# A two-layer decoder trunk on one core, with its instruction order worked out by the framework's finer model of engines and queues

## The chip, the core and the metric

The kernel runs on one core of a Trainium2 chip. A core has a matrix engine (TensorE, PE in the profile), three engines for elementwise work (VectorE = DVE, ScalarE = ACT, GpSimd = POOL) and SyncE (SP), whose queue here issues every DMA. Each engine takes its own instructions in the order in which they stand in its list, and waits at the head of that list for what the head instruction needs. The metric is device time in microseconds (us) of the whole program, median over runs; lower is better.

## The reference, cut to what matters

The model has two layers with 256 tokens and 2048 channels, all in 32-bit floats. Each layer is a token mixer and a SwiGLU feed-forward network (FFN), and both are modulated by a conditioning vector `c`:

```
c_act = silu(c)
for l in range(2):
    mod = c_act @ w_mod[l] + b_mod[l]                  # 2048 -> 6 * 2048
    shift1, scale1, gate1, shift2, scale2, gate2 = split(mod, 6)
    h = rms_norm(x) * (1 + scale1) + shift1
    x = x + gate1 * mixer(h, w_in[l], ..., w_out[l])    # three head groups in parallel
    h = rms_norm(x) * (1 + scale2) + shift2
    x = x + gate2 * ((silu(h @ w_gate[l]) * (h @ w_up[l])) @ w_down[l])
return rms_norm(x)
```

The mixer's three groups are gated linear attention (`gla`), sliding-window attention (`swa`) and a gated delta rule (`gdn`). The delta rule inverts a triangular matrix in a series of dependent small products. Per layer the weights hold 40.1 MB (`w_in`), 16.8 MB (`w_out`), 138 MB (gate, up and down) and 100.7 MB (`w_mod`, 2048 x 12288), so that a quarter of the bytes that the kernel reads serve only the vector `mod`.

## The kernel before

**Weights for TensorE.** `stream` (line 293 on) handles every large product. It walks over weight tiles of 128 rows and 1024 columns, 512 KB each. A tile is loaded by SP into `raw` (line 323, three buffers). ACT makes its rounded part `wh` (line 330, three buffers) and DVE the remainder `wl` (line 331, three buffers). TensorE then runs twelve products per tile (line 358): two column halves, two blocks of 128 tokens, three terms. A `raw` buffer is free again once its `wl` is made. In layer 0's mixer most tiles are used whole (`whole`): they skip the split, land in any of the `raw`, `wh` and `wl` buffers, and cost TensorE one slower product in place of three.

**The modulation vector.** `mod_segment` (line 201 on) handles `c_act @ w_mod`. DVE multiplies a loaded tile of `w_mod` with one value of `c_act` per row and adds it to `acc` (line 223). In the first part (shift1 and scale1 of layer 0) the tiles are 512 columns wide and take buffers of the mixer's pool (`g`, 256 KB, line 220). All others are 1024 columns wide and have two buffers of their own (`mraw`, 512 KB, line 220); their sums have two buffers (`acc`). Sixteen such tiles make a segment, which TensorE and ACT or DVE then finish (lines 234 to 256, `fin`).

**What sets the order.** The kernel calls its operations in one sequence. `tick` (line 273) is called after each weight tile and puts steps of the modulation between them, at a rate set by hand for each stage (`RATE_IN`, `RATE_FFN` and so on). The framework's scheduler then takes this sequence, plays the instructions through a model of the machine, and from it makes the list of each engine: an instruction whose inputs and buffers are there in the model may pass an earlier one that is still waiting. No semaphore, buffer or instruction is written out by hand; the lists follow from the model.

Stages by time in the profiled execution: first modulation segments until 41 us, layer 0's input projections and mixer until about 575 us, its FFN until about 1372 us, layer 1's projections and mixer until about 1816 us, and its FFN to the end. The gdn's inversion (lines 673 to 692, in `gdn`) is made of rounds of four small products (line 678), a masked copy on DVE (680), four products (685), a subtraction on DVE (686), four transposes (403) and a copy on ACT (687).

The few lines on which the steps rest:

```
rawp = tile_pool(name="rawp", bufs=3)       # weight tiles as loaded
modp = tile_pool(name="modp", bufs=2)       # w_mod tiles, "mraw"
wsp  = tile_pool(name="wsp", bufs=3)        # wh and wl, three each
accp = tile_pool(name="accp", bufs=2)       # sums of two segments
SY.dma_start(raw, w_mod[...])               # line 220
V.scalar_tensor_tensor(acc, raw, c_act, acc, mult, add)   # line 223
SY.dma_start(raw, w[k])                     # line 323
A.activation(wh, raw, Copy)                 # line 330
V.tensor_tensor(wl, raw, wh, subtract)      # line 331
TE.matmul(ps, x, wh or wl)                  # line 358
```

The function that the change touches:

## Time and profile before

| | us |
|---|---|
| median of 3 runs (2581.72 to 2582.03) | 2581.92 |
| the profiled execution, whole | 2585.34 |
| its span, first to last instruction | 2583.5 |
| TensorE busy in the span | 2432.7 (94%) |
| DVE busy | 1714.4 (66%) |
| ACT busy | 1053.5 (41%) |

The DMA engines read 596.63 MB, on average 232 GB/s over the span. Idle time is counted by engine; a view by time windows gives for each stretch how long each engine was busy, how many instructions it ran (x...), the share of time in which the sixteen DMA engines were busy, and the rate in GB/s. The same view for one tile's name counts only the instructions that touch that tile: `mraw` on DVE counts the modulation's products, `raw` on DVE counts the weight splits.

### The profile page before, as it was taken

How to read it: one execution, taken by the hardware profiler on the slowest of the kernel's cores; microseconds unless marked ns; L12 is line 12 of the kernel's file. 1: busy time of each engine (PE TensorE's matmuls, PEld its weight loads, DVE VectorE, ACT ScalarE, POOL GpSimd, SP SyncE). 2: the span in 40 equal slices, each digit the busy share in tenths (PEclk: the TensorE clock that was granted, in tenths of full speed). 3: DMA queues.
4: the chain of work that ended last, by engine and by line, in shares of the span. 5: the costliest groups of instructions: out<-in, count | busy, mean ns of one | idle time of the engine just before them, and what ended most of it. 6: DMA issues, size and time to landing. Idle time of an engine off the chain costs nothing.

```text
span 2583.5 us, 30803 instructions
## 1 busy us (share of the span) xinstructions
PE 2432.7 (94%) x11164; PEld 1884.1 (73%) x11164; DVE 1714.4 (66%) x2171; ACT 1053.5 (41%) x1548; POOL 58.2 (2%) x117
## 2 busy tenths in 40 slices
PE   4999998889999988999999999999999999999998
PEld 2555785447878767788877878877778878888876
DVE  6767867576675777657578785888664575544555
ACT  2203443124444333344335454564644434344443
POOL 1000000000000000000000000000000000000000
PEclk9999999989999999999999999999999999999999
DMA  9996538777778888868687861675676686666654
GB/s 341 368 322 204 180 114 282 258 231 268 261 259 260 283 268 274 292 193 286 223 277 261 281 192 50 214 232 192 212 256 193 200 286 195 188 191 188 189 184 155
DMA packets 190033, 600.79 MB, mean 233 GB/s; under 512 B 21628, under 2 KB 26268, under 8 KB 189496
## 3 DMA queue, kind: packets, MB, share of 16 engines
q1 hardware_dynamic: 189880, 598.81, 70.7%
q8 instruction: 88, 1.44, 0.2%
q14 instruction: 65, 0.53, 0.1%
HBM read 596.63 MB, written 2.10 MB: 232 GB/s over the span
## 4 chain that ended last, share of the span: by engine, by line
PE 57%; DMA 20%; DVE 10%; issue 8%; ACT 4%; POOL 1%; SPq 1%; DVEq 0%; ACTq 0%; POOLq 0%
PE acc L358 48%; DMA mraw<-in_w_mod 13%; DVE wl L331 4%; DMA raw<-in_w_down 3%; DMA raw<-in_w_in 2%; DVE acc L223 2%; ACT wh L330 1%; PE mm L403 1%; PE ga L895 1%; DMA raw<-in_w_up 1%; PE mm L678 1%; PE mm L685 1%; PE ga L916 1%; DMA raw<-in_w_gate 1%; PE fin L248 1%
## 5 line engine op out<-in xcount | busy, mean ns | idle before, releaser
L358 PE MATMUL acc<-wh,hm 128*128 128x512 f32 (+3 forms) x4872 | 1339.2, 389 | 20.9 <-DVE xs L931 4.7
L330 ACT ACTIVATE wh<-raw 128x1024 fp32r<-128x1024 f32 (+3 forms) x669 | 684.7, 1025 | 985.8 <-PE acc L358 548.9
L331 DVE TENSOR_TENSOR wl<-raw,wh 128x1024 fp32r<-128x1024 f32 (+3 forms) x669 | 785.2, 1179 | 446.6 <-ACT wh L330 444.5
L358 PEld LDWEIGHTS acc<-wh,hm 128*128 128x128 f32 x4872 | 892.0, 189 | 215.8 <-issue 25.5
L358 PE MATMUL acc<-wl,hm 128*128 128x512 f32 (+3 forms) x2484 | 792.3, 394 | 12.2 <-DVE wl L331 9.7
L223 DVE SCALAR_TENSOR_TENSOR acc<-mraw,c_act,acc 128x1024 f32<-128x1024 f32 x320 | 410.3, 1282 | 225.2 <-DMA mraw<-in_w_mod 222.9
L358 PEld LDWEIGHTS acc<-wl,hm 128*128 128x128 f32 x2484 | 458.4, 190 | 124.1 <-DVE wl L331 22.3
L358 PE MATMUL acc<-wh,ahl 128*128 128x512 f32 x560 | 158.4, 397 | 0.0
L358 PEld LDWEIGHTS acc<-wh,ahl 128*128 128x128 f32 x560 | 105.8, 189 | 24.5
L358 PE MATMUL acc<-wl,ahl 128*128 128x512 f32 x280 | 90.8, 398 | 7.2 <-DVE wl L331 7.2
L223 DVE SCALAR_TENSOR_TENSOR g<-g,c_act,g 128x512 f32<-128x512 f32 x128 | 88.7, 747 | 12.6 <-DMA g<-in_w_mod 12.4
L358 PE MATMUL acc<-wh,b 128*128 128x512 f32 (+2 forms) x184 | 74.7, 545 | 2.2 <-ACT b L447 2.1
L358 PE MATMUL acc<-wl,b 128*128 128x512 f32 (+2 forms) x176 | 67.1, 518 | 2.6 <-DVE g L969 2.6
L358 PEld LDWEIGHTS acc<-wl,ahl 128*128 128x128 f32 x280 | 52.2, 189 | 23.1 <-DVE wl L331 11.3
L358 PE MATMUL acc<-raw,b 128*128 128x512 f32 (+2 forms) x176 | 67.6, 524 | 0.0
L358 PEld LDWEIGHTS acc<-wh,b 128*128 128x128 f32 x184 | 35.2, 197 | 30.8 <-issue 23.1
L358 PEld LDWEIGHTS acc<-wl,b 128*128 128x128 f32 x176 | 32.8, 192 | 29.2 <-issue 20.3
L416 ACT ACTIVATE acc<-xs 128x512 f32<-128x512 f32 x32 | 19.0, 595 | 85.7 <-DVE xs L931 85.7
L447 ACT ACTIVATE b<-mm,mod,mod 128x128 f32<-128x128 f32 x24 | 9.2, 461 | 109.7 <-DVE mod L256 92.1
L358 PEld LDWEIGHTS acc<-raw,b 128*128 128x128 f32 x176 | 33.5, 195 | 26.7 <-issue 21.7
L929 DVE TENSOR_TENSOR acc<-acc,gate 128x512 f32<-128x512 f32 x64 | 43.0, 695 | 10.3 <-PE acc L358 10.2
L358 PE MATMUL acc<-raw,hm 128*128 128x512 f32 x88 | 41.7, 598 | 1.4 <-ACT acc L416 1.4
(314 smaller groups left out, 1645.8 us busy)
## 6 DMA issues: line engine op xcount, KB each, us to landing
mraw<-in_w_mod SPq DMA_DIRECT2D x320, 512.0 KB
raw<-in_w_down SPq DMA_DIRECT2D x176, 512.0 KB
raw<-in_w_gate SPq DMA_DIRECT2D x160, 512.0 KB
raw<-in_w_up SPq DMA_DIRECT2D x160, 512.0 KB
raw<-in_w_in SPq DMA_DIRECT2D x72, 512.0 KB
g<-in_w_mod SPq DMA_DIRECT2D x128, 256.0 KB
raw<-in_w_out SPq DMA_DIRECT2D x43, 512.0 KB
raw<-in_w_in SPq DMA_DIRECT2D x32, 264.0 KB
```

Of the source, the lines that this page charges most:

```text
L223: V.scalar_tensor_tensor(acc, raw[:, a], c_act[:, i + a:i + a + 1], acc, ALU.mult, ALU.add)
L248: TE.transpose(ps[:, i * P:(i + 1) * P], acc[:, (j + i) * P:(j + i + 1) * P], ident)
L330: A.activation(wh[:, :width], raw[:, :width], AF.Copy)
L331: V.tensor_tensor(wl[:, :width], raw[:, :width], wh[:, :width].bitcast(F32), ALU.subtract)
L358: TE.matmul(ps[blk, j][:, :segs[j][2]], xa, parts[j][part], start=i == 0 and n == 0, stop=last and n == len(terms) - 1)
L403: TE.transpose(ps[:, j * P:(j + 1) * P], src[:, j * P:(j + 1) * P], ident)
L416: A.activation(scr[0]() if junk is None else junk, xs[:, blk, j * 512:(j + 1) * 512], AF.Square, accum_out=ssq[blk][:, j:j + 1])
L678: TE.matmul(ps[:, s], LT[blk][:, s], Tm[blk][:, s], start=True, stop=True)
L685: TE.matmul(ps[:, s], U[blk][:, s], m1[:, s], start=True, stop=True)
L895: TE.matmul(ps[:, j * nk:(j + 1) * nk], qT[rows, i + j], kT[rows, g, :nk], start=True, stop=True)
L916: TE.matmul(ps[:, j * 64:(j + 1) * 64], pT[:, j * nk + kb * P:j * nk + (kb + 1) * P], kv[kb][:, P + g * 64:P + (g + 1) * 64], start=kb == ...
L929: V.tensor_tensor(ps, ps, need(gate_row, (l, part, j)), ALU.mult)
```

## The change

```diff
-    with tile.TileContext(nc) as tc:
+    with tile.TileContext(nc, schedule_with_timeline_sim=True) as tc:
         trunk(tc, *args)
```

On SP's list, at the very start: loads for the first modulation segments (`g`, from `w_mod`) and the first weights (`wh`, `wl`, `raw`, from `w_in`). Before:

```order
L220 DMA g_60_232<-in_w_mod 128x512
L220 DMA g_61_235<-in_w_mod 128x512
L220 DMA g_62_238<-in_w_mod 128x512
L220 DMA g_63_241<-in_w_mod 128x512
L220 DMA g_64_244<-in_w_mod 128x512
L220 DMA g_65_247<-in_w_mod 128x512
```

Now:

```order
L220 DMA g_60_232<-in_w_mod 128x512
L323 DMA wh_96_347<-in_w_in 128x1024
L323 DMA wl_106_372<-in_w_in 128x1024
L323 DMA raw_110_387<-in_w_in 128x1024
L323 DMA wh_114_402<-in_w_in 128x1024
L323 DMA wl_119_424<-in_w_in 128x520
L220 DMA g_61_235<-in_w_mod 128x512
```

Before, all 32 `g` loads of the first two segments stood ahead of the first weight. Now ten loads of `w_in` (3.55 MB) and four of `mraw` (2.1 MB) stand among them.

On SP's list in layer 0's FFN, at the gate projection that was read at about 780 us: weight tiles (`raw`) and the modulation's tiles (`mraw`). Before:

```order
L323 DMA raw_1339_5553<-in_w_gate 128x1024
L323 DMA raw_1342_5571<-in_w_gate 128x1024
L323 DMA raw_1345_5589<-in_w_gate 128x1024
L323 DMA raw_1355_5628<-in_w_gate 128x1024
L323 DMA raw_1358_5646<-in_w_gate 128x1024
L323 DMA raw_1362_5667<-in_w_gate 128x1024
```

Now:

```order
L323 DMA raw_1339_5553<-in_w_gate 128x1024
L220 DMA mraw_1564_6710<-in_w_mod 128x1024
L323 DMA raw_1342_5571<-in_w_gate 128x1024
L213 DMA acc_1663_7259<-in_b_mod 1x1024
L220 DMA mraw_1574_6767<-in_w_mod 128x1024
L323 DMA raw_1345_5589<-in_w_gate 128x1024
L220 DMA mraw_1581_6806<-in_w_mod 128x1024
L323 DMA raw_1355_5628<-in_w_gate 128x1024
L220 DMA mraw_1591_6863<-in_w_mod 128x1024
L323 DMA raw_1358_5646<-in_w_gate 128x1024
```

The modulation's tiles now come one for nearly every weight tile. From `raw_1065` (read at 596 us) to `raw_1964` (at 1234 us) the list held 110 `mraw` loads and now holds 181, beside the same weights: 171.0 MB before, 208.2 MB now. From layer 1's first input weight (`raw_2158`) to its first gate weight (`raw_3129`) it held 64 and now holds none. The whole lists hold the same loads.

On TensorE's list in layer 0's gdn, one round of the inversion and the beginning of the next (`mm`: the round's products; `acc` from `wh` and `wl`: input projections; `ga`: attention). Before:

```order
L678 MATMUL mm_476_1719<-g_470_1693,g_466_1681 128x128 x4
L358 MATMUL acc_678_2497<-wh_702_2608,hm_289_993 128x512
L358 MATMUL acc_679_2498<-wh_702_2608,hm_289_993 128x512
L358 MATMUL acc_676_2493<-wh_706_2629,hm_190_657 128x512
L358 MATMUL acc_677_2494<-wh_706_2629,hm_190_657 128x512
L358 MATMUL acc_676_2493<-wl_707_2630,hm_190_657 128x512
L685 MATMUL mm_478_1726<-g_477_1724,g_469_1690 128x128 x4
```

Now:

```order
L678 MATMUL mm_476_1719<-g_470_1693,g_466_1681 128x128 x4
L916 MATMUL ga_608_2247<-kv_151_533,b_606_2240 128x64
L916 MATMUL ga_608_2247<-kv_152_538,b_606_2240 128x64
L916 MATMUL ga_608_2247<-kv_151_533,b_606_2240 128x64
L916 MATMUL ga_608_2247<-kv_152_538,b_606_2240 128x64
L685 MATMUL mm_478_1726<-g_477_1724,g_469_1690 128x128 x4
L895 MATMUL ga_610_2255<-kT_412_1425,b_585_2170 128x256 x2
```

The input projections that stood between the rounds now all stand ahead of the first of them. From the first round's products to the gdn's last transposes TensorE's list held 118 products of projections, and now holds 26 (of `w_out`). On DVE's list the same rounds held 9 modulation products and now hold 31.

## The prediction

> **What bounds the kernel now.** I read the page first: TensorE's share, the slices and the chain that ended last.

> ```profile
> span 2583.5 us, 30803 instructions
> PE 2432.7 (94%) x11164; PEld 1884.1 (73%) x11164; DVE 1714.4 (66%) x2171; ACT 1053.5 (41%) x1548; POOL 58.2 (2%) x117
> GB/s 341 368 322 204 180 114 282 258 231 268 261 259 260 283 268 274 292 193 286 223 277 261 281 192 50 214 232 192 212 256 193 200 286 195 188 191 188 189 184 155
> PE 57%; DMA 20%; DVE 10%; issue 8%; ACT 4%; POOL 1%; SPq 1%; DVEq 0%; ACTq 0%; POOLq 0%
> PE acc L358 48%; DMA mraw<-in_w_mod 13%; DVE wl L331 4%; DMA raw<-in_w_down 3%; DMA raw<-in_w_in 2%; DVE acc L223 2%; ACT wh L330 1%; PE mm L403 1%; PE ga L895 1%; DMA raw<-in_w_up 1%; PE mm L678 1%; PE mm L685 1%; PE ga L916 1%; DMA raw<-in_w_gate 1%; PE fin L248 1%
> ```

> TensorE is busy 94% of the span, so a better order can win at most 150 us. The second link of the chain matters here: 13% of it is the landing of `mraw`, tiles that no weight product needs soon. A change of order moves exactly these tiles. So I cut the program into stages, and counted the modulation's products in them (the same view, for `mraw` alone) and the weight splits (for `raw` alone).

> ```profile
> core 0: us, PE busy (x) PEld busy (x) DVE busy (x) ACT busy (x) POOL busy (x), PEclk, DMA share, GB/s
> 40.80:228.00 187.20, 183.75 (x554) 101.21 (x554) 132.96 (x239) 30.37 (x68) 2.73 (x16) 0.99 0.95 337
> 371.00:575.00 204.00, 180.92 (x759) 105.16 (x760) 144.87 (x202) 52.58 (x114) 7.94 (x8) 0.96 0.80 263
> 596.00:861.00 265.00, 256.11 (x1131) 206.76 (x1130) 179.13 (x161) 113.05 (x121) 1.91 (x2) 1.00 0.82 274
> 861.00:1041.00 180.00, 165.54 (x702) 131.08 (x701) 128.56 (x122) 61.01 (x61) 1.90 (x2) 0.97 0.83 271
> 1372.00:1694.00 322.00, 309.49 (x1853) 260.76 (x1853) 241.81 (x401) 166.04 (x319) 13.95 (x31) 1.00 0.62 199
> 1694.00:1816.00 122.00, 112.73 (x582) 88.08 (x582) 102.69 (x146) 67.49 (x114) 4.46 (x4) 0.99 0.62 204
> 596.00:1245.00 649.00, 623.52 (x2732) 503.26 (x2731) 438.08 (x399) 259.69 (x270) 4.77 (x5) 0.99 0.81 268
> ```

> Modulation products (`mraw`), three stages, then weight splits (`raw`):

> ```profile
> 861.00:1041.00 180.00, 0.00 (x0) 0.00 (x0) 47.47 (x37) 0.00 (x0) 0.00 (x0) 0.97 0.83 271
> 1372.00:1694.00 322.00, 0.71 (x2) 0.30 (x2) 64.52 (x52) 1.25 (x2) 0.00 (x0) 1.00 0.62 199
> 1694.00:1816.00 122.00, 1.98 (x6) 1.05 (x6) 19.22 (x16) 1.16 (x2) 0.00 (x0) 0.99 0.62 204
> ...
> 861.00:1041.00 180.00, 0.00 (x0) 0.00 (x0) 68.89 (x57) 59.22 (x57) 0.97 0.83 271
> 2150.00:2550.00 400.00, 0.00 (x0) 0.00 (x0) 174.95 (x144) 151.37 (x143) 1.00 0.61 189
> ```

> The last row is the pace that TensorE sets when nothing disturbs it: 144 tiles in 400 us, 2.78 us per weight tile, at 189 GB/s. In 861 to 1041 us, 57 tiles took 180 us, 3.16 us each, with 37 modulation tiles beside them. TensorE ran 702 products there; in 2150 to 2550 it runs 1761 in 400 us, so 792 in 180. A ninth was lost. The rate was only 271 GB/s. Why it is no higher, the timeline of that stretch shows:

> ```profile
> 886.95 0.33 SPq L323 DMA_DIRECT2D raw<-in_w_down  x1
> 890.42 1.28 DVE L223 SCALAR_TENSOR_TENSOR acc<-mraw,c_act,acc 128x1024 f32<-128x1024 f32 x1 [3.49 <-DMA mraw<-in_w_mod]
> 891.73 0.33 SPq L220 DMA_DIRECT2D mraw<-in_w_mod  x1
> 891.94 1.06 ACT L330 ACTIVATE wh<-raw 128x1024 fp32r<-128x1024 f32 x1 [1.70 <-DMA raw<-in_w_down]
> 893.22 1.28 DVE L223 SCALAR_TENSOR_TENSOR acc<-mraw,c_act,acc 128x1024 f32<-128x1024 f32 x1 [0.38 <-DMA mraw<-in_w_mod]
> 894.42 1.22 DVE L331 TENSOR_TENSOR wl<-raw,wh 128x1024 fp32r<-128x1024 f32 x1
> ```

> SP issued nothing from 887.3 to 891.7 us: the next load on its list, an `mraw`, waited for DVE to free its buffer, and DVE had waited 3.49 us for the `mraw` before it. The weight loaded at 886.95 landed by 891.94, ACT took 1.06, and its `wl` stood behind a modulation product until 894.42, so the buffer was free at 895.64: 8.7 us round trip for one of three buffers. The loop of five buffers through SP's and DVE's strict lists sets the rate, not TensorE. SP's waits in nearly the same window say it in sum:

> ```profile
> SPq L323 <- DVE wl L331: 120.5, 61, 4.2
> SPq L220 <- DVE acc L223: 13.3, 12, 1.4
> ```

> **The change, part by part.** The sum is made against the profiled execution (2585.3 us with what lies around its span), which is 3.4 us above the median of the runs shown.

> 1. *Start.* The first product on weights is here:

> ```profile
> 5.32 26.05 SPq L220 DMA_DIRECT2D g<-in_w_mod  x31
> 40.83 2.08 PE L358 MATMUL acc<-wh,b 128*128 128x512 f32 x2 [2.09 <-ACT b L447]
> ```

> It needs the last of 32 `g` loads. The new list puts 5.65 MB ahead of that load. At the second slice's 368 GB/s that is 15 us; if the weights only fill time in which SP waited for `g` buffers, the 2.1 MB of `mraw` remain, 6 us. TensorE is then full (183.75 of 187.20 us in the first row of the stage table), so what is lost stays lost until some idle time takes it back. I take +10 (6 to 15).

> 2. *Layer 0's mixer.* The gdn's rounds lose their cover: 118 - 26 = 92 products of the projections now run earlier, and 22 more modulation products stand between the rounds on DVE. Their price if each holds the chain up, by the 1.28 us above, is 28 us; with 92 products of 0.23 us (400 us / 1761) uncovered, 21 more, together 49. Against that, 371 to 575 us has 23 us of idle TensorE, where `w_out` waited; those products come earlier in the new list, too. What runs earlier is no less work, so a gain is bounded by these 23. I take +5 (-20 to +49), near nothing since DVE's load over the stage is the same.

> 3. *Layer 0's FFN, 596 to 1245 us.* The same weights (221 splits) now come with 181 modulation tiles for 110: 208.2 MB. If the rate stays the 271 GB/s of the stretch that is most like it, this takes 768 us for 649: +119. If the queue can be filled to a share of 1.00, the rate is 271 / 0.83 = 327 GB/s and the stage takes 637 us: -12. The best single window that TensorE filled is this:

> ```profile
> 1170.00:1235.00 65.00, 64.98 (x295) 53.63 (x294) 51.11 (x47) 27.07 (x28) 0.00 (x0) 1.00 0.90 302
> ```

> Sustained 302 would give 689 us, +40. I take the mean of 271 and 302, 286 GB/s: 728 us, +79. DVE gets 71 more products, 91 us on 438 of 649: no bound by itself, but each stands ahead of some `wl`. What waits behind a late `wl` is SP's next weight load three tiles on.

> [...]

> 4. *Rest of layer 0's FFN (1245 to 1372 us):* 9 `mraw` loads for 14. -5 (-8 to 0).

> 5. *Layer 1's mixer (1372 to 1816 us):* its modulation is done already. 68 products go, 84 us of DVE's 344. TensorE idles 22 us by the two rows; the norms and the gdn chain keep a part of it. Here, too, the projections move ahead of the last rounds. -10 (-22 to +15).

> 6. *Layer 1's FFN* keeps its 32 modulation tiles in all, a little earlier; 0. From 2150 us on the lists load the same tiles in the same order; that stretch must not change.

> Sum: 10 + 5 + 79 - 5 - 10 = +79. 2585.3 + 79 = 2664, less 3.4 is **2661 us**.

> **The rivals.**

> *A. The loop is not the limit (faster).* With an `mraw` always next to a weight, all five buffers are in flight and the rate goes up, as it did at the start (337 GB/s over 187 us, where the loads had more buffers). Break-even is 208.2 MB / 649 us = 321 GB/s; above it TensorE's pace decides, 221 x 2.78 = 614 us, -35. For it: the DMA share of 0.83 leaves room. Against: that share already went with 271 GB/s. At 327 GB/s: +10 + 0 - 12 - 5 - 20 = -27, about 2555 us by the median.

> *B. The bare gdn chains cost, too (slower still).* Each modulation product between two rounds waits for its tile's landing, and with it DVE and the chain. Layer 0 then pays its 49 instead of 5, layer 1 gains nothing: 79 + 44 + 10 = 133, 2715 us. For it: 22 more products among the rounds. Against: one attention block's work still lies between them.

> *C. Gains and losses meet.* At 308 GB/s the FFN loses 27 (676 us) and its rest gains 5; layer 1 gains its 22, the start costs 6 and layer 0's mixer gains 6: 0, 2582 us. For it: all terms but one are small.

> That the lists don't differ is excluded: they do.

> **How the numbers follow.** The forecast's case has 0.68, A 0.12, B 0.16, C 0.04. The likeliest case alone runs from 2610 (FFN at 302 GB/s, layer 1 at its best) to 2700 (271 GB/s). With C below and the larger part of B above, 8 in 10 lie in 2580 to 2730. A change under 0.2%, 5 us, is about what this measurement can't tell from none. Faster: A, 0.12 (C's sides cancel). Same: C, 0.04. Slower: 0.84.

> **What would show it.** In the new profile, layer 0's FFN (to be found by its first gate weight and layer 1's first `w_in` weight) should be some 75 us longer; its windows should show 275 to 300 GB/s, TensorE near 85%, and ACT's `wh` waiting for the landing of `raw`. The first product on weights should start near 51 us. Layer 1's mixer should show no `mraw` and a rate under 140 GB/s. The last 430 us should look as before. If layer 0's FFN shows over 320 GB/s and a full TensorE, step 3 is wrong and the kernel is faster; if the FFN is as predicted and the total is not, the mixers' steps are.

## The result, and the profile after

The changed kernel is slower: 2720.19 us (median of 4 runs, 2717.2 to 2721.98) against 2581.82 us, a ratio of 1.054 (95% interval 1.0522 to 1.0559). The forecast was 2661 us in a range of 2580 to 2730: the sign and the range hold, the sum is 59 us short. The profiled execution took 2720.07 us.

The page of the changed kernel gives the span and the engines' busy time:

```profile
span 2718.3 us, 30932 instructions
PE 2484.0 (91%) x11164; PEld 1946.1 (72%) x11164; DVE 1719.4 (63%) x2171; ACT 1058.8 (39%) x1551; POOL 55.8 (2%) x117
```

The span grew by 134.8 us. TensorE ran the same 11164 instructions, but was busy 51.3 us longer (2484.0 for 2432.7). So it was idle 83.5 us longer, and what it ran took longer. The mean clock that TensorE was granted fell from 0.986 of the full one to 0.959. The prediction had no term for that second part.

To see where the time went I take the start of the first product that uses the same weight tile, in both traces:

| up to the first product on | before, us | after, us | stretch longer by |
|---|---|---|---|
| the first weight tile | 40.8 | 55.7 | +15 |
| a tile late in layer 0's projections (`wl_675`) | 237.7 | 258.6 | +6 |
| layer 0's second gate pair (`raw_1065`): the mixer | 603.4 | 666.3 | +42 |
| `raw_1964`: most of layer 0's FFN | 1245.0 | 1342.3 | +34 |
| layer 1's first input weight (`raw_2158`) | 1372.5 | 1475.3 | +6 |
| layer 1's first gate weight (`raw_3129`): the mixer | 1816.5 | 1940.1 | +21 |
| near the end (`raw_4067`) | 2526.7 | 2662.9 | +13 |

Windows of the kernel before over layer 0's mixer and FFN (us, busy time of PE, PEld, DVE, ACT, POOL with counts, then clock, DMA share, GB/s):

```profile
238.00:603.00 365.00, 331.94 (x1618) 225.88 (x1616) 256.59 (x408) 131.43 (x299) 19.23 (x24) 0.95 0.63 203
603.00:1245.00 642.00, 617.38 (x2704) 498.52 (x2705) 433.50 (x395) 258.03 (x269) 4.77 (x5) 0.99 0.81 268
```

The same stages of the changed kernel, and layer 1's mixer in two pieces:

```profile
259.00:666.00 407.00, 353.91 (x1625) 252.14 (x1624) 248.58 (x407) 143.13 (x311) 18.95 (x24) 0.89 0.53 168
666.00:1342.00 676.00, 629.78 (x2747) 511.36 (x2746) 523.82 (x481) 258.01 (x269) 10.51 (x11) 0.97 0.89 308
1475.00:1700.00 225.00, 222.43 (x1203) 189.96 (x1203) 130.59 (x240) 121.60 (x201) 4.16 (x5) 0.98 0.54 153
1700.00:1940.00 240.00, 211.15 (x1208) 174.18 (x1206) 139.40 (x235) 109.39 (x222) 6.17 (x13) 0.93 0.31 95
```

Three things stand in these rows. Layer 0's mixer holds nearly the same products and takes 42 us more: 22 of them are TensorE's products at a lower clock (353.91 us at 0.89 for 331.94 at 0.95; if the busy time goes with the clock, I estimate from these rows 315 us at a clock of 1.00 for both), 20 are idle. Layer 0's FFN moves 308 GB/s, more than the 286 that the forecast took, so it loses less. In layer 1's mixer TensorE is nearly full for 225 us, and idle for 29 of the 240 us behind them, at a clock of 0.93; its projections are used up by 1735 us, and the products of `w_out` start near 1795. (The sizes at the head of this document make `w_mod` 201 of the 597 MB that are read: a third, not a quarter.)

The 20 idle us lie in the rounds of layer 0's inversion, from the first product of line 678 to the last. These rounds in the kernel before:

```profile
288.60:344.90 56.30, 56.30 (x383) 48.00 (x382) 40.15 (x57) 24.47 (x52) 2.14 (x5) 1.00 0.40 122
```

and in the changed kernel, with DVE's longest wait there (us in total, times, longest):

```profile
374.40:458.20 83.80, 63.70 (x362) 49.85 (x361) 61.26 (x77) 17.93 (x47) 2.99 (x7) 0.88 0.69 210
DVE acc L223 <- DMA mraw<-in_w_mod: 19.0, 22, 2.3
```

The rounds take 84 us for 56. Among them DVE now runs 30 modulation products (38.5 us; 7 before) and waits 19 us for the landing of their tiles (not at all before). Its busy time and these waits fill 80 of the 84 us.

### The profile page after: what moved, and what is told of

The parts are those of the page before. It is cut to its first block, busy times and chain, and to the rows that moved or that the text cites. A ratio compares the mean times of both kernels' runs of the same rounds, so it can differ in the third digit from the quotient of the medians.

```text
span 2718.3 us, 30932 instructions
## 1 busy us (share of the span) xinstructions
PE 2484.0 (91%) x11164; PEld 1946.1 (72%) x11164; DVE 1719.4 (63%) x2171; ACT 1058.8 (39%) x1551; POOL 55.8 (2%) x117
## 4 chain that ended last, share of the span: by engine, by line
PE 56%; DMA 23%; DVE 11%; ACT 5%; issue 4%; SPq 0%; POOL 0%; DVEq 0%; ACTq 0%; POOLq 0%
PE acc L358 49%; DMA mraw<-in_w_mod 15%; DVE acc L223 4%; DVE wl L331 3%; ACT wh L330 2%; DMA raw<-in_w_up 2%; DMA raw<-in_w_down 2%; DMA raw<-in_w_gate 1%; DMA g<-in_w_mod 1%; DMA raw<-in_w_in 1%; DVE acc L929 1%; PE mm L403 1%; PE ga L895 1%; DVE g L223 1%; PE ga L403 1%
## 5 line engine op out<-in xcount | busy, mean ns | idle before, releaser
L358 PE MATMUL acc<-wh,hm 128*128 128x512 f32 (+3 forms) x4872 | 1357.7, 391 | 32.9 <-DVE xs L931 17.1
L331 DVE TENSOR_TENSOR wl<-raw,wh 128x1024 fp32r<-128x1024 f32 (+3 forms) x669 | 785.4, 1179 | 530.1 <-ACT wh L330 527.1
L358 PEld LDWEIGHTS acc<-wh,hm 128*128 128x128 f32 x4872 | 906.3, 191 | 234.5 <-issue 39.1
L330 ACT ACTIVATE wh<-raw 128x1024 fp32r<-128x1024 f32 (+3 forms) x669 | 683.8, 1026 | 985.8 <-PE acc L358 499.1
L358 PE MATMUL acc<-wl,hm 128*128 128x512 f32 (+3 forms) x2484 | 808.6, 395 | 9.8 <-DVE wl L331 8.1
L358 PEld LDWEIGHTS acc<-wl,hm 128*128 128x128 f32 x2484 | 464.8, 192 | 120.2 <-issue 17.1
L223 DVE SCALAR_TENSOR_TENSOR acc<-mraw,c_act,acc 128x1024 f32<-128x1024 f32 x320 | 410.2, 1282 | 158.0 <-DMA mraw<-in_w_mod 156.2
L358 PE MATMUL acc<-wh,ahl 128*128 128x512 f32 x560 | 156.4, 395 | 0.0
L358 PEld LDWEIGHTS acc<-wh,ahl 128*128 128x128 f32 x560 | 105.5, 188 | 24.7
L223 DVE SCALAR_TENSOR_TENSOR g<-g,c_act,g 128x512 f32<-128x512 f32 x128 | 89.7, 746 | 19.5 <-DMA g<-in_w_mod 13.6
L358 PE MATMUL acc<-wl,ahl 128*128 128x512 f32 x280 | 90.5, 397 | 0.8 <-DVE wl L331 0.8
L358 PE MATMUL acc<-wh,b 128*128 128x512 f32 (+2 forms) x184 | 78.1, 535 | 4.0 <-ACT b L447 4.0
L358 PE MATMUL acc<-raw,b 128*128 128x512 f32 (+2 forms) x176 | 73.2, 526 | 2.0 <-ACT b L447 1.5
L358 PE MATMUL acc<-wl,b 128*128 128x512 f32 (+2 forms) x176 | 72.5, 522 | 1.5 <-ACT b L447 1.5
L358 PEld LDWEIGHTS acc<-wl,ahl 128*128 128x128 f32 x280 | 52.1, 188 | 14.6 <-DVE wl L331 2.8
L358 PEld LDWEIGHTS acc<-wh,b 128*128 128x128 f32 x184 | 35.4, 194 | 34.2 <-issue 26.5
L358 PEld LDWEIGHTS acc<-raw,b 128*128 128x128 f32 x176 | 33.5, 193 | 29.5 <-issue 23.8
L358 PEld LDWEIGHTS acc<-wl,b 128*128 128x128 f32 x176 | 33.6, 195 | 27.9 <-issue 23.2
L447 ACT ACTIVATE b<-mm,mod,mod 128x128 f32<-128x128 f32 x24 | 9.0, 457 | 102.6 <-DVE mod L256 98.7
L358 PE MATMUL acc<-raw,hm 128*128 128x512 f32 x88 | 42.9, 611 | 0.0
L931 DVE TENSOR_TENSOR xs<-xs,acc 128x512 f32<-128x512 f32 x64 | 41.7, 680 | 0.3
```

The costliest lines, as they stand in the source:

```text
L223: V.scalar_tensor_tensor(acc, raw[:, a], c_act[:, i + a:i + a + 1], acc, ALU.mult, ALU.add)
L330: A.activation(wh[:, :width], raw[:, :width], AF.Copy)
L331: V.tensor_tensor(wl[:, :width], raw[:, :width], wh[:, :width].bitcast(F32), ALU.subtract)
L358: TE.matmul(ps[blk, j][:, :segs[j][2]], xa, parts[j][part], start=i == 0 and n == 0, stop=last and n == len(terms) - 1)
L447: A.activation(h32[:, i], ps[:, i * P:(i + 1) * P], AF.Identity, scale=mod_col[l, 3 * sub + 1, at + i], bias=mod_col[l, 3 * sub, at + i])
L931: V.tensor_tensor(x_j, x_j, ps, ALU.add)
```

## The experiments

Most runs fix the order of issue on some engines. Every instruction has the same name in all these programs, so an engine's list can be taken from one kernel and laid on another: each instruction is tied behind the one ahead of it on its engine, an order of issue without a wait. Engines that are not tied get their lists from the finer model, worked out anew beside the tied ones; such a list need not be the changed kernel's.

```diff
+    known = {i.name: i for i in nc.cur_bb.bb.instructions}
+    for packed in lists:
...
+        for a, b in zip(names, names[1:]):
+            tc.add_manual_dep(known[b], a, mybir.DependencyInfo(
+                mybir.DependencyClass.NoSync, mybir.DependencyReason.DATA), reason="pin")
```

All results by stage, against the kernel before, in us and in the stretches of the table above (start and projections; layer 0's mixer; its FFN; the FFN's rest; layer 1's mixer; its FFN), with the ratio of times:

| run | start | mixer 0 | FFN 0 | rest | mixer 1 | FFN 1 | ratio (95%) |
|---|---|---|---|---|---|---|---|
| the change | +21 | +42 | +34 | +6 | +21 | +13 | 1.054 (1.0522 to 1.0559) |
| loads_before | 0 | +71 | +26 | +13 | +79 | +16 | 1.0748 (1.0723 to 1.0773) |
| pe_before_mods_free | +53 | +17 | +19 | +5 | +2 | +5 | 1.0434 (1.0402 to 1.0465) |
| pe_before | +28 | +34 | -5 | +6 | +45 | +2 | 1.0446 (1.0422 to 1.047) |
| products_in_call_order | +43 | +46 | +15 | +4 | +34 | +15 | 1.0656 (1.0624 to 1.0688) |
| only_PE_free | +9 | +76 | +2 | +5 | +60 | +16 | 1.0666 (1.0623 to 1.071) |
| only_DVE_free | +6 | +35 | +12 | +10 | +49 | +14 | 1.0493 (1.0463 to 1.0523) |
| only_mod_products_free | +5 | +24 | +16 | +9 | +27 | +6 | 1.0333 (1.0315 to 1.0351) |
| only_other_DVE_free | +3 | +19 | -1 | +1 | +18 | +10 | 1.0187 (1.0166 to 1.0208) |
| mod_products_in_call_order | +10 | +134 | -21 | +1 | +72 | +8 | 1.0792 (1.0769 to 1.0814) |
| only_SP_free | +15 | +5 | -30 | -2 | -2 | 0 | 0.9967 (0.9948 to 0.9986) |
| start_before_rest_of_SP_free | +13 | +1 | -25 | -3 | +3 | -2 | 0.994 (0.9924 to 0.9956) |
| SP_free_from_the_FFN_on | -2 | -1 | -29 | -2 | +1 | -1 | 0.9867 (0.9844 to 0.9891) |

**First: loads against TensorE's order.** Three runs, all with the finer model for what is not tied.

```diff
+        pin(tc, nc, (SP_BEFORE,))
```

> The order in which SP issues the loads is that of the kernel before, instruction for instruction; the other lists are worked out by the finer model, so that TensorE's input projections still run ahead of the delta rule's rounds (20 projection products among layer 0's rounds, against 74 before and 16 in the changed kernel). Theory 1, from the two traces: the start (+15), the K-block stage (+6) and layer 0's FFN (+34) lose by the order of the loads, and the two mixers (+42 and +21) by the bare rounds. Then the first three go and the mixers' 63 us stay: 2635 to 2670 us. Rival, as in the prediction: all that is lost hangs on the modulation's loads, and bare rounds cost next to nothing: 2580 to 2600 us.

Measured: 2778.94 us. The start is back (first weight product at 39.9 us), so the start's loss is made by the loads' order. But the whole became slower than the changed kernel. The mixers lose 150 us, and the FFN loses 26 with every load where it stood before. Neither theory had that: the old list of loads, with the lists that the finer model works out around it, is slower than both kernels.

```diff
+        pin(tc, nc, (PE_BEFORE,))
```

Here `PE_BEFORE` leaves the products of lines 238 and 248 (`fin`) out.

> TensorE's list is that of the kernel before in all but the 160 small products that finish a modulation segment; the rest is by the finer model. The rounds of the delta rule have their cover of projections again (74 products, as before), while the modulation's loads stand nearly as in the changed kernel: 179 of them in layer 0's FFN against 181 (110 before), none in layer 1's mixer, 27 modulation products on DVE among layer 0's rounds against 30. Theory 1: start, K-blocks and FFN keep their loss of about 55 us, the mixers lose little: 2635 to 2670 us. Rival (the loads' order is all): 2700 to 2725 us. If modulation products among the rounds are what stretches layer 0's mixer, not the lack of cover, its 42 us stay and the time is near 2685 us.

Measured: 2697.37 us. The mixers fall to +17 and +2, from +42 and +21, with nearly the changed kernel's modulation. So 44 of the mixers' 63 us go with TensorE's old list, in which the projections stand among layer 0's rounds again. In layer 0 this gives back the clock, and not the idle time. This run's windows over layer 0's mixer, over its rounds, and over what lies behind them:

```profile
291.00:674.00 383.00, 330.72 (x1613) 224.31 (x1612) 224.81 (x370) 130.45 (x292) 16.91 (x23) 0.95 0.51 160
363.60:445.60 82.00, 63.96 (x395) 51.75 (x394) 65.43 (x81) 22.69 (x48) 2.66 (x4) 0.96 0.67 209
445.60:674.10 228.50, 214.68 (x987) 135.67 (x986) 97.42 (x182) 84.12 (x192) 7.83 (x13) 1.00 0.39 123
```

and the changed kernel behind its rounds:

```profile
458.20:666.30 208.10, 179.80 (x673) 114.35 (x673) 95.56 (x169) 64.93 (x149) 7.05 (x9) 0.85 0.34 108
```

TensorE is busy for 330.72 us at 0.95, as in the kernel before (331.94), not 353.91 at 0.89. But it is idle for 52 us, as in the changed kernel (53; 33 before), and the rounds take 82 us with their cover of projections, for 84 without: DVE has 28 modulation products in them and waits 15.8 us for the tiles. So their length does not come from the missing cover. The start, 32 us worse than the changed kernel's, ate about half of what the other stages gained.

```diff
+        pin(tc, nc, (PE_BEFORE,))
```

> TensorE's whole list is that of the kernel before, the small products that finish a modulation segment among them; SP, DVE and ACT are ordered by the finer model. Since a segment's buffer comes free only behind those products, the loads fall back to nearly their old places (112 in layer 0's FFN, 62 in layer 1's mixer); what stays of the change is the start, with 20 modulation tiles ahead of time, and DVE's and ACT's order. Theory 1: start and K-blocks only, 2590 to 2610 us. Rival: the finer model's order on DVE (the splits against the modulation's products) costs by itself in every stage: over 2620 us.

Measured: 2699.64 us, against theory 1. TensorE's list is the old one to the last instruction, the loads are nearly back, and yet the mixers lose 34 and 45 us. Layer 0's rounds are not where: without a modulation product among them they are as short as in the kernel before.

```profile
332.80:389.20 56.40, 56.30 (x383) 47.92 (x382) 30.07 (x47) 23.35 (x50) 1.21 (x4) 1.00 0.19 57
```

This run and the one before it issue TensorE's products in the same order, all but the `fin` products. So 26 us of the rounds go with the modulation products on DVE. The clock over this run's whole mixer is 0.93, so the cover alone does not keep it up. What the mixers still lose here points to DVE's or ACT's order.

**Second: one engine at a time.** TensorE's list of the changed kernel holds something that the prediction had missed: 4570 of the 8616 weight products stand out of the sequence in which the kernel calls them (464 before).

```diff
-                TE.matmul(ps[blk, j][:, :segs[j][2]], xa, parts[j][part],
-                          start=i == 0 and n == 0, stop=last and n == len(terms) - 1)
+                put = TE.matmul(ps[blk, j][:, :segs[j][2]], xa, parts[j][part],
+                                start=i == 0 and n == 0, stop=last and n == len(terms) - 1)
+                if prods:
+                    tc.add_manual_dep(put.ins, prods.pop().name, mybir.DependencyInfo(
+                        mybir.DependencyClass.NoSync, mybir.DependencyReason.DATA), reason="pin")
+                prods.append(put.ins)
```

> The changed kernel, with one constraint: TensorE issues the weight products (line 358) in the sequence in which the kernel calls them. The finer model had moved 4570 of the 8616 from their place in that sequence (464 in the kernel before); at a group's first tiles it does one column half of three tiles in a row, and holds all three tiles' buffers open. Everything else stays as in the changed kernel, nearly: 180 modulation loads in layer 0's FFN, none in layer 1's mixer, the input projections ahead of the delta rule's rounds. Theory 2, new: the moved products cost layer 0's FFN most of its 29 us, and some of the mixers': 2680 to 2700 us, FFN (first gate weight to the layer's last-but-one weight tile) 10 us or less above the kernel before. Rival, step 3 of the prediction: the 71 additional modulation tiles cost the FFN its time; it keeps 25 to 35 us, and the whole stays at 2710 to 2725 us.

Measured: 2748.8 us. The FFN did as theory 2 says in kind (+15 for +34, with 180 modulation tiles still), but the start lost 22 us more and layer 1's mixer 13, so the whole is slower. The moved products cost the FFN some 19 us; undoing them cost more elsewhere, and the mixers kept their loss.

```diff
+        pin(tc, nc, (DVE_BEFORE, ACT_BEFORE, SP_BEFORE))
```

> SP's, DVE's and ACT's lists are those of the kernel before, instruction for instruction; TensorE's alone is worked out by the finer model. It keeps the projections among the delta rule's rounds (the other lists tie them), but moves 4884 of the 8616 weight products from their call order. Theory 2: this alone costs layer 0's FFN 10 to 25 us and the kernel 20 to 50: 2600 to 2635 us. Rival: the sequence of products within a tile or two is indifferent, since their sum is the same: 2580 to 2590 us.

Measured: 2752.69 us, far beyond both. The freed list stays near the old one, with the projections still among the rounds, and yet it costs the mixers 136 us (the FFN 2).

```diff
+        pin(tc, nc, (PE_BEFORE, SP_BEFORE, ACT_BEFORE))
```

> TensorE's, SP's and ACT's lists are those of the kernel before; DVE's alone is worked out by the finer model, which sets modulation products and attention work ahead of the delta rule's convolution (line 548) and of weight splits, by two places on average. Theory 3: DVE's order is what stretches the mixers even where TensorE's list is the old one (they lost 37 and 38 us in the run with TensorE's whole list as before): 2605 to 2650 us, with the loss in the two mixers. Rival: two places are too little to matter: 2580 to 2590 us, and the mixers' loss in that run came from the loads and ACT.

Measured: 2706.4 us. DVE's list moved by under two places on average, and the kernel lost 125 us, in all stages. The mixers' loss is theory 3's; its size is double the expectation.

```diff
+        pin(tc, nc, (PE_BEFORE, DVE_BEFORE, ACT_BEFORE))
```

> TensorE's, DVE's and ACT's lists are those of the kernel before; SP's alone is worked out by the finer model: 9 loads of weights and modulation stand ahead of the last early modulation loads at the start, and the two kinds of loads are mixed otherwise by 2.7 places on average. Step 1 of the prediction and theory 1: the start costs 10 to 20 us and the rest next to nothing, 2590 to 2605 us. Rival: loads that stand in another order than the engines use them stop SP at a buffer that comes free late, all along the kernel: over 2620 us.

Measured: 2572.45 us, 0.3% faster than the kernel before. The start costs what theory 1 said, and layer 0's FFN gains 30 us, which no theory had.

These three results (DVE alone costs 125 us, TensorE alone 171, SP alone gains 9) are not parts of the change's 138 us. On average an instruction of the freed lists stands 2 (DVE), 8 (TensorE) and 3 (SP) places from where it stood before; in the changed kernel's lists it is 49, 63 and 33. So they show what a small change of order on one engine can cost, not what the change's own lists cost one by one. ACT alone was not freed.

**Third: what on DVE.** The 320 modulation products alone, and then everything but them.

```diff
+        pin(tc, nc, (PE_BEFORE, SP_BEFORE, ACT_BEFORE, DVE_OTHERS_BEFORE))
```

> TensorE's, SP's and ACT's lists are those of the kernel before, and DVE's, too, in all but the 320 modulation products on the wide tiles (line 223): these alone find their place by the finer model. They move up by a few places, ahead of 107 weight splits, of 61 products of the delta rule's convolution and of attention and residual work. Theory 3: the finer model counts a tile as landed earlier than it lands on the chip, so DVE waits at its product while work that is ready stands behind it: most of the 125 us that DVE's free list cost comes back, 2660 to 2710 us, with DVE's waits for these landings at 290 us or more (223 before). Rival: the convolution and the attention work, which stay here, cost it: 2580 to 2605 us.

```diff
+        behind(tc, nc, MODS_BEHIND)
+        pin(tc, nc, (PE_BEFORE, SP_BEFORE, ACT_BEFORE))
```

> The complement: TensorE's, SP's and ACT's lists as before, each modulation product behind the instruction that stood ahead of it on DVE before; the rest of DVE's list is by the finer model, so that attention's rotations and some splits stand ahead of the delta rule's convolution (line 548), as in the run in which DVE alone was free. Theory 3: 2580 to 2605 us. Rival: 2660 to 2710 us, with the loss at the convolution, early in the mixers.

Measured: 2669.83 and 2633.77 us, so 85 and 49 us; their sum of 134 is near the 125 of DVE's whole list. Each is part of the truth. DVE's waits for the landing of modulation tiles over the whole span (engine, line, what it waited for: us in total, times, longest) in the kernel before:

```profile
DVE acc L223 <- DMA mraw<-in_w_mod: 222.9, 170, 4.0
```

and in the run with the modulation products alone free:

```profile
DVE acc L223 <- DMA mraw<-in_w_mod: 310.3, 228, 4.5
```

In the run with the other instructions free they come to 212.5 us. With the modulation products free that is 87 us more of waiting, and 85 us more of time. Stage by stage, too: in the order of the table the waits grow by 4, 22, 22, 5, 28 and 6 us, the stages by 5, 24, 16, 9, 27 and 6. The products stand ahead of splits, convolution and attention work that is ready, and hold it up until their tile has landed. That the finer model takes the tiles as landed sooner than the chip lands them is my reading of it; the runs show only where it puts the products and what that costs. The 49 us of the other instructions lie in the two mixers (+19 and +18) and layer 1's FFN; which of them cost it (attention ahead of the convolution, line 548, is the largest group that moved) was not taken apart.

```diff
-                V.scalar_tensor_tensor(acc, raw[:, a], c_act[:, i + a:i + a + 1], acc,
-                                       ALU.mult, ALU.add)
+                tc.keep_in_program_order(V.scalar_tensor_tensor(
+                    acc, raw[:, a], c_act[:, i + a:i + a + 1], acc, ALU.mult, ALU.add))
```

> The changed kernel, with one constraint: each modulation product stands on DVE behind what the kernel calls ahead of it on that engine. Its loads then can't run ahead either: 91 in layer 0's FFN (181 in the changed kernel, 110 before), 82 from layer 0's first output weight to its first gate weight (42), 94 in layer 1's mixer (none). TensorE's list stays of the new kind, with the projections ahead of the rounds. Theory 3 taken to the changed kernel: what the early modulation costs goes, 15 to 20 us in the FFN and some in layer 0's mixer, and the bare rounds stay: 2680 to 2710 us. Rival: in the changed kernel all lists were worked out together, and holding one kind of instruction back puts them out of step: slower than it, over 2725 us.

Measured: 2788.93 us, the rival's side. Theory 3 could not be carried to the changed kernel in this form. The FFN gained 55 us against the changed kernel (-21 for +34) with 91 tiles for 181, some 0.6 us for each tile less, if all of it is theirs. But the mixers lost 134 and 72 us: with the products held back, the FFN's shift and scale were not ready at the end of layer 0's mixer. TensorE's list is not the expected one either: 71 products of projections stand among layer 0's rounds (16 in the changed kernel, 74 before), so the bare rounds were not kept. With no modulation product among them these rounds take 77 us, in which TensorE is busy for 69: modulation is not the only thing that can stretch them. TensorE's waits from 352 to 748 us of this run, and its window at the end of layer 0's mixer:

```profile
PE fin L248 <- issue: 86.2, 3, 41.3
```

```profile
640.00:748.00 108.00, 34.77 (x137) 27.40 (x136) 58.23 (x58) 19.25 (x41) 2.63 (x3) 0.61 0.58 175
```

Three waits ahead of the products that finish a segment took 86 us, two of them (25 and 41 us) in this window, in which TensorE was busy for 35 of 108 us.

**Fourth: the loads by themselves.** The gain in the run with SP alone free is a place where the finer model does better than the other. Two runs ask where it is made.

```diff
+        pin(tc, nc, (PE_BEFORE, DVE_BEFORE, ACT_BEFORE, SP_MIXED))
```

> TensorE's, DVE's and ACT's lists are those of the kernel before. SP's list begins as in the kernel before, up to the last of the first 32 modulation loads (g); behind it the loads stand as in the run in which SP alone was free. That run lost 11 us up to the first weight product and won 30 in layer 0's FFN. If both belong to the places where they show, the start is back at 40 to 41 us and the time near 2560 us (2555 to 2568), faster than both kernels. If the early weights were what the later gain lived on (more loads ahead from the start), the gain shrinks with them: 2570 to 2582 us.

Measured: 2569.2 us, between the two expectations. The FFN's gain stayed (-25), the start came back by only 3 us of 11: the first weight product began at 48.9 us. Ten `w_in` loads and two `mraw` now stand right behind the 32 `g` loads, where weights and further `g` loads had alternated. So the first of those further `g` tiles lands later, and DVE's old list has its product ahead of the last step of the second segment (line 256), for which the weights' first products wait:

```profile
47.44 0.75 DVE L223 SCALAR_TENSOR_TENSOR g<-g,c_act,g 128x512 f32<-128x512 f32 x1 [8.21 <-DMA g<-in_w_mod]
48.10 0.16 DVE L256 SCALAR_TENSOR_TENSOR mod<-sums,gains 128x4 f32<-128x4 f32 x1
```

The 8.21 us of this wait are the 8 us that remain of the loss.

The last run has the same edit, with `SP_MIXED` as before up to the first gate weight.

> TensorE's, DVE's and ACT's lists are those of the kernel before, and SP's up to layer 0's first gate weight; from there on SP's loads stand as in the run in which SP alone was free, where a modulation load stands about one weight load earlier than before (112 of them in layer 0's FFN, for 110). That run won 33 us from the first gate weight to layer 1's first input weight, and lost 18 before it. If the gain is made by these loads alone, the first gate weight is used at 566 us as before and the time is 2545 to 2556 us, with DVE's waits for modulation tiles near 140 us (223 before). If it hung on work that the earlier stages had done ahead, 2570 to 2585 us.

Measured: 2550.83 us, 1.3% faster than the kernel before, and as expected; DVE's waits for the tiles fell further than expected, to 104.5 us for some 140. SP's list of loads in layer 0's FFN, in the kernel before:

```
L323 DMA raw_1431_6024<-in_w_up 128x1024
L220 DMA mraw_1487_6296<-in_w_mod 128x1024
L323 DMA raw_1446_6082<-in_w_down 128x1024
L220 DMA mraw_1497_6353<-in_w_mod 128x1024
L323 DMA raw_1454_6107<-in_w_down 128x1024
```

and in this run:

```
L323 DMA raw_1431_6024<-in_w_up 128x1024
L220 DMA mraw_1497_6353<-in_w_mod 128x1024
L323 DMA raw_1446_6082<-in_w_down 128x1024
L323 DMA raw_1454_6107<-in_w_down 128x1024
L220 DMA mraw_1504_6392<-in_w_mod 128x1024
```

`mraw_1497` is issued one weight load earlier; DVE uses it where it did. Of the stage's 110 modulation loads 52 stand one weight load earlier, 18 two or more, and 37 where they stood. DVE's waits from 596 to 1245 us in the kernel before:

```profile
DVE wl L331 <- ACT wh L330: 104.5, 82, 4.1
DVE acc L223 <- DMA mraw<-in_w_mod: 101.5, 79, 3.6
```

and in the same stretch of this run:

```profile
DVE wl L331 <- ACT wh L330: 158.5, 141, 2.5
DVE acc L223 <- DMA mraw<-in_w_mod: 28.9, 29, 2.5
```

Its window over layer 0's FFN:

```profile
601.00:1214.00 613.00, 606.94 (x2706) 497.34 (x2704) 434.25 (x397) 257.63 (x268) 4.77 (x5) 1.00 0.83 281
```

The wait for the landing is mostly gone from DVE, which now waits for ACT's rounded part more often but shorter (1.1 us instead of 1.3 each). TensorE is busy 606.94 of 613 us: the FFN runs at TensorE's pace, 221 tiles at the prediction's 2.78 us, 614 us.

## Why the prediction was right and where it was not

The sign was right, and the range held. That the sum came as near as it did is partly luck: the FFN was put 45 us too high, and the other stages together 103 us too low. By its own steps:

1. *Start, +10 (6 to 15).* Measured +15 at the first product on weights, and +6 more through the projections. With the loads as before (loads_before) both are gone, so the cause is the one given. The upper bound was the right value: all 5.65 MB ahead of the last `g` load counted, not only the `mraw` part. By the traces DVE has the second segment's sum 13.5 us later, and two modulation products that now stand ahead of the segment's last step make up most of the rest.

2. *Layer 0's mixer, +5 (-20 to +49).* Measured +42. The text had a price for the modulation products among the rounds, 28 us, and set it aside because DVE's load over the stage is the same. In the rounds it is not, and the price was paid: they take 27 us longer. With the cover in place they were as long (82 us), and with the cover and no modulation among them as short as before (56 us). The other price, 21 us for uncovered products, did not come as waiting: 82 and 84 us are nearly the same. What goes with the moved products is the clock: behind the rounds it reads 0.85 (179.80 busy us) for 0.95 in the kernel before (229.44 busy us from 344.9 to 603 us). If the busy time goes with the clock, I estimate that at some 15 us (179.80 x 0.15 less 229.44 x 0.05), for which no term was there; with TensorE's old list (pe_before_mods_free) the clock reads 1.00 there.

3. *Layer 0's FFN, +79 (-12 to +119).* Mis-sized: +34. The step took 286 GB/s, the mean of two windows of the old list, as what a loop of five buffers can carry. The stage ran at 308: with its loads in other places the same loop carried more. Of the 34 us 22 are idle time and 12 longer products. The runs take the +34 apart, as an estimate from their differences, which holds only if these add up: loads that stand earlier gain 30 (only_SP_free, 112 tiles), some 70 tiles more cost 45 (products_in_call_order, 180 tiles, at +15), and the moved weight products cost 19 (from +15 to +34). The step had the second of these only. Its reading of the wait (SP held at a buffer, since DVE waits for a landing) was right, and the last run is that reading put to use (DVE's waits for landings in this stage fell there to 28.9 us from 101.5).

4. *Rest of the FFN, -5.* Measured +6: five `mraw` fewer, no gain.

5. *Layer 1's mixer, -10 (-22 to +15).* Measured +21, outside the bounds. It does without modulation (0 products), at 123 GB/s as forecast. But the projections ran ahead, and the second half of the rounds was bare: 10 of the 21 us are idle time, 11 longer products at a lower clock (433.28 busy us at 0.96 for 422.22 at 0.99). With TensorE's old list it lost 2. The 84 us of DVE's work that left the stage were worth nothing: that run, too, has no modulation there, and gains nothing.

6. *Layer 1's FFN, 0.* Measured +13; 10 of them behind the tile that was first used at 2134 us, in the stretch that was not to change. The loads there have the same order, but more than half of TensorE's products have another. That this is the cause is only argued: the two runs with TensorE's old list and free DVE and ACT lost 2 and 5 here, but the call order alone (+15) did not help, and DVE's list alone costs 14.

Rival A put the FFN at TensorE's pace. It came to that pace in the last run, not in the changed kernel. Rival B's number, 2715 us, is the nearest, in part by luck, since its term for the FFN is the forecast's. Its mechanism is what layer 0's rounds show: DVE waits there 19.0 us for the landing of modulation tiles, and the chain with it. It is not the whole: over the whole kernel these waits fell, from 222.9 to 156.2 us, layer 1's rounds hold no modulation, and the clock is not in it. Rival C had the FFN to the number (308 GB/s, 676 us), but its gains elsewhere did not come.

What the sum could not show is that its terms are not independent. DVE's load over a stage does not say what stands behind a product that waits for its tile, and a place on one engine's list has its price only beside the other lists. Why a list of TensorE that stays so near the old one costs the mixers 76 and 60 us stays open.

## What to carry to other kernels

Where an in-order engine waits at an operation for its data while ready work stands behind it, issue that load one or two places earlier and leave the operation where it is: here the order of the loads alone, from the first FFN on, was worth 1.3%. Work that waits for a stream did harm here among the steps of a dependent chain, though the engine's load over the stage stayed nearly the same (DVE busy 248.58 us for 256.59): with 30 products in place of 7 the rounds took 84 us for 56. Independent dense work beside chains of small products may be worth more than its own time: behind the rounds the granted clock read 0.85 where it was gone and 1.00 in pe_before_mods_free, where it stood. That the cover alone keeps the clock up is not shown: pe_before has it, too, and its whole mixer reads 0.93. And do not judge a new order by one engine's list. Freeing one list beside fixed ones helps to find what costs, but a list made in that way is another one than the change's.

## What the hardware showed that was not expected

TensorE was busy for 12.44 of 13 us at a granted clock of 0.50. In the changed kernel the gated linear attention of layer 0 ran with no large products beside it. Windows of that stage (the clock is the third number from the end):

```profile
570.00:583.00 13.00, 12.44 (x72) 11.66 (x71) 11.88 (x25) 5.04 (x8) 0.00 (x0) 0.50 0.00 0
568.00:602.00 34.00, 25.24 (x124) 22.88 (x125) 17.44 (x37) 9.22 (x21) 1.01 (x1) 0.50 0.00 0
598.50:602.00 3.50, 3.50 (x16) 3.50 (x17) 0.00 (x0) 0.00 (x0) 0.00 (x0) 0.50 0.00 0
```

The 12.44 us (first window) went to products of 64 rows and 128 columns. From 602.4 us on the clock reads 1.00. By then TensorE had run 3.5 us of products of 128 rows and 128 columns without a break (lines 840 and 842, the last window), and 0.4 us of the first products of 128 by 512. The same line in the kernel before, from 415 to 566 us, with `w_out` products between:

```profile
L823 PE MATMUL ga<-a 64*128 64x128 f32 x56 | 8.0, 283 | 2.7 <-DVE a L804 2.5
```

and in the changed kernel, from 364 to 634 us:

```profile
L823 PE MATMUL ga<-a 64*128 64x128 f32 x56 | 13.6, 415 | 4.6 <-DVE a L831 4.6
```

283 ns became 415 ns each; the 48 of them that ran from 568 to 602 us, at 0.50, took 437 ns. What sets the clock these rows do not show. It stayed at 0.50 over 12.44 busy us of products of 64 rows, and reads 1.00 behind 3.5 us of products that were as narrow but had 128 rows. Whether the rows of a product decide it is a guess from one case, and was not tried.
